# One extra multiply of ones ahead of the seven-product streams of four FFNs

## The chip, the cores and the metric

The kernel runs on one core of a Trainium2 chip. The metric is the device time of one execution in microseconds (us), median of several runs, lower is better. Three runs of the kernel before took 1838.65, 1840.2 and 1842.27 us; the median is 1840.2 us. Engines are named as in the profile: PE is the matrix engine (PEld its weight loads), DVE the vector engine, ACT the activation engine, POOL GpSimd, SP the engine that issues the weight transfers.

## The reference

Two batches of 256 tokens with 1024 channels go through a trunk of two layers with the same weights, so the kernel works on 512 tokens at once. Each layer is a half-step FFN, a token mixer, a second half-step FFN and a norm:

```python
def swiglu(x, w_gate, w_up, w_down):
    return (jax.nn.silu(x @ w_gate) * (x @ w_up)) @ w_down

for layer in range(DEPTH):                      # DEPTH = 2
    x = x + 0.5 * swiglu(rms_norm(x, ffn1_norm[layer]), ...)
    h = rms_norm(x, mix_norm[layer])
    x = x + mixer(h)                            # attention, another kind in each layer
    x = x + 0.5 * swiglu(rms_norm(x, ffn2_norm[layer]), ...)
    x = rms_norm(x, final_norm[layer])
```

The FFN's inner width is 2816, which is 22 chunks of 128. All is float32. The change touches only the four FFNs, called FFN1 to FFN4 here in order of time.

## The kernel before

**Products.** PE multiplies in a rounded float32 type, so every operand is split in a high and a low part (`wh`, `wl` for weights, `xh`, `xl` or pieces of `xb` for tokens), and each block product is three matmuls: `wh` by `xh`, `wh` by `xl`, `wl` by `xh`. ACT writes `wh` as a rounded copy, and DVE writes `wl` as the difference. Both read either a raw weight tile (`raw`, filled by a DMA on SP's queue, two buffers) or a sum of weight blocks (`T`, made by DVE).

**An FFN.** `ffn()` handles its 22 chunks in groups of 4, 6, 6 and 6 (`GROUPS`). For each chunk f it makes gate and up values, and after each group follows a down projection of that group (512-wide matmuls, `ba<-ah,wh` and the like, added up into X). The first chunks of an FFN (three in FFN1, two in the others, `PLAIN`) are made by plain 512-wide products. All other chunks take gate and up together by a Strassen-like scheme of seven products, numbered m = 1 to 7, on halves of the tokens: each has four blocks of 128 rows by three matmuls, which makes 12 matmuls of 256 columns. The products of a chunk run in the order 1, 3 (of the chunk before), 7, 6, 2, 5, 4. A group of six chunks is 42 products, 504 matmuls. In the first chunk by seven products (f = `PLAIN`) product 1 stands between the plain products, and the stream proper begins with product 6.

**Banks.** Products accumulate in banks of the matrix engine's result memory: `ba` (two, by chunk parity; products 1 and 2), `bg` (product 7), `bb` (two; products 4 and 6), `bc` (two; products 3 and 5). ACT copies `ba` into `bb` after product 1 and `bb` into `bc` after product 6, so that later products add to them; `gs<-bg` saves product 7; DVE forms `gate` and `us` from the banks, and the results are split into `ah` and `al` for the down projection. Products 1 and 7 begin with `start=True`, which overwrites the bank. An older piece, `begin()` (lines 877 to 880), multiplies a tile of ones by itself into the first halves of `bb` and `bc` at the start of each FFN, four matmuls of 256 columns.

**Order.** The order of PE's work is fixed by `ffn_order` (line 197 on). The order on ACT and DVE is worked out while the program is built: `Plan.run` (line 463 on) has an estimated clock per engine (`Clock`, `Engine.cost`), every PE product has a due time, and whichever ready task with the nearest due time is handed out next, weight copies (`emit_hi`), weight differences (`emit_lo`) and sums (`emit_sum`) among them. An engine runs its instructions strictly in the order so handed out, and waits at the first whose input is missing. The estimated clock advances with every call that goes through the `Engine` helper, so an extra matmul moves it too. All instructions show line 151, the helper's line.

Of the kernel before, what the change touches and what calls it, by code (L numbers as in the profile page):

```python
# [15 lines left out]
P = 128  # L16
# [5 lines left out]
GROUPS = (4, 6, 6, 6)  # L22
# [3 lines left out]
XSIDE = {1: 0, 7: 1, 2: 2, 4: 3, 6: 4, 3: 5, 5: 6}  # L26
# [3 lines left out]
PLAIN = {True: 3, False: 2}  # L30
# [512 lines left out]
def hybrid_trunk_kernel(ctx, tc, x, cst, wgu1, wd1, wgu2, wd2, win_ab, wout_ab, win_c, wout_c, ali, nab, y):  # L543
# [5 lines left out]
    PE = Engine(clock, "pe", nc.tensor)  # L549
# [11 lines left out]
    def acc(name):  # L561
        return clock.alloc(acc_p.tile([P, T], F32, tag="acc", name=name), "acc", BANKS["acc"])
# [72 lines left out]
    ones_r = per.tile([P, P], F32R, name="ones")  # L635
# [218 lines left out]
    def ffn(norm, nxt, index, groups, boundary=None, before=()):  # L854
        with tc.tile_pool(name="ffn", bufs=2, reuse_waits="tile") as fp:
            plan = Plan(clock, ws)
            l_first = bool(before)
            ba = [acc("ba") for _ in range(2)]
            bg = acc("bg")
            bb = [scp("bb") for _ in range(2)]  # L860
            bc = [trp("bc") for _ in range(2)]
            half = slice(0, 256)
# [7 lines left out]
            norm.more = [a.rearrange("p (k i t) -> p k i t", k=4, i=3) for a in shared("xb", F32R)]  # L870
            acts = {}
            part = {}

            steps = plan.steps
            steps(before)
# [8 lines left out]
            def when(do):  # L884
                later.append(do)
                if "S" in plan.writer:
                    while later:
                        later.pop(0)()
# [2 lines left out]

            def multiply(f, m, ps):
                wh, wl = ws.ready[index[f, WSIDE[m]]]
                for k in range(4):
                    w = slice(k * P, (k + 1) * P)
                    xh, xl = norm.block(XSIDE[m], k)
                    for j, (wt, xt) in enumerate(((wh, xh), (wh, xl), (wl, xh))):
                        PE.matmul(ps[:, half], lhsT=wt[:, w], rhs=xt, start=(m in (1, 7) and k == 0 and j == 0),
                                  stop=(k == 3 and j == 2), skip_group_check=True)

            def product_of(f, m):
                i = f % 2
                a, b, c = ba[i], bb[i], bc[i]
                ka, kb, kc = f"a{i}", f"b{i}", f"c{i}"
                gate, us, gs = f"gate{i}", f"us{i}", f"gs{i}"
                ps, key = {1: (a, ka), 2: (a, ka), 3: (c, kc), 4: (b, kb), 5: (c, kc), 6: (b, kb), 7: (bg, "g")}[m]
                p = index[f, WSIDE[m]]
                plan.add("pe", lambda: multiply(f, m, ps), [f"x{k}{XSIDE[m]}" for k in range(4)], [key], 1.404, (p, p + 1))
                if m == 1:
                    plan.add("act", lambda: A.activation(b[:, half], a[:, half], AF.Copy), [ka], [kb], 0.27)  # L910
                elif m == 7:
                    def keep():
                        part[f, "s"] = t = fp.tile([P, 256], F32, tag="gs", name="gs")
                        A.activation(t, bg[:, half], AF.Copy)
                    plan.add("act", keep, ["g"], [gs], 0.27)
                elif m == 6:
                    plan.add("act", lambda: A.activation(c[:, half], b[:, half], AF.Copy), [kb], [kc], 0.27)
                elif m == 2:
                    def scale():
                        part[f, "g"] = t = fp.tile([P, T], F32, tag="gate", name="gate")  # L920
                        V.tensor_tensor(t[:, half], a[:, half], norm.wide["s"][:, half], ALU.mult)
                    when(lambda: plan.add("dve", scale, [ka, "S"], [gate, gate + "b"], 0.34))
                elif m == 5:
                    def total():
                        part[f, "u"] = t = fp.tile([P, 256], F32, tag="us", name="us")
                        V.tensor_tensor(t, c[:, half], part[f, "s"], ALU.add)
                    plan.add("dve", total, [kc, gs], [us], 0.34)
                elif m == 4:
                    def total():
                        V.tensor_tensor(part[f, "g"][:, second], b[:, half], part.pop((f, "s")), ALU.add)  # L930

                    def scale():
                        t = part[f, "g"]
                        V.tensor_tensor(t[:, second], t[:, second], norm.wide["s"][:, second], ALU.mult)

                    def finish():
                        plan.add("dve", total, [kb, gs], [gate + "b"], 0.34)
                        plan.add("dve", scale, ["S"], [gate + "b"], 0.34)
                        plan.add("act", lambda: A.activation(part[f, "g"], part[f, "g"], AF.Silu), [],
                                 [gate, gate + "b"], 0.53)  # L940
                    when(finish)
                elif m == 3:
                    def times(s, what):
                        t = part[f, "g"]
                        V.tensor_tensor(t[:, s], t[:, s], what(), ALU.mult)

                    plan.add("dve", lambda: times(second, lambda: part.pop((f, "u"))), [us], [gate + "b"], 0.34)
                    plan.add("dve", lambda: times(half, lambda: c[:, half]), [kc], [gate], 0.34)
                    split_acts(f)
# [42 lines left out]
            def split_acts(f):  # L992
                gate = f"gate{f % 2}"

                def high():
                    t = fp.tile([P, T], F32R, tag="ah", name="ah", bufs=NA)
                    A.activation(t, part[f, "g"], AF.Copy)
                    part[f, "h"] = t

                def low():  # L1000
                    t = fp.tile([P, T], F32R, tag="al", name="al", bufs=NA)
                    h = part.pop((f, "h"))
                    V.tensor_tensor(t, part.pop((f, "g")), h.bitcast(F32), ALU.subtract)
                    acts[f] = (h, t)
                plan.add("act", high, [gate, gate + "b"], [f"ah{f % NA}"], 0.53)
                plan.add("dve", low, [f"ah{f % NA}", gate + "b"], [f"al{f % NA}", gate], 0.61)
# [88 lines left out]
            for slot, (kind, f, *m) in enumerate(order):  # L1095
                if slot == 3:
                    steps(stats)
                    steps(spread[:-2])
                    for k in range(4):
                        steps(norm.block_steps(k, room, False))  # L1100
                    late = [norm.block_steps(k, room, True) for k in range(4)]
                    for begun, _ in late:
                        steps(begun)
                if slot == 5:
                    steps(spread[-2:])
                    when(lambda: None)
                    steps(again[:-2])
                if slot == 6:
                    steps(again[-2:])
                if kind == "m" and f == n0 and m[0] == 6:  # L1110
                    for _, ended in late:
                        steps(ended)
                if kind == "m":
                    product_of(f, m[0])
                elif kind != "down":
                    plain(f, kind, m[0])
                else:
                    down(f, GROUPS[f], f0)
                    f0 += GROUPS[f]
            plan.run()  # L1120
            p = groups[-1][-1]
# [655 lines left out]
    before = [step for c in range(KC) for step in n.feed_steps(c)]  # L1777
    for l in range(2):
        for which in range(3):
            if which == 0:  # L1780
                nx = Norm(gains(1, l))
                ffn(n, nx, *ffn_parts[2 * l], gains(3, 0) if l == 1 else None, before if l == 0 else ())
            elif which == 1:
                nx = Norm(gains(2, l))
                (mixer_ab if l == 0 else mixer_c)(n, nx)
            else:
                if l == 0:
                    nx = Norm([comb[:, c:c + 1] for c in range(KC)], gains(3, 0))
                else:
                    nx = Last(gains(3, 1))  # L1790
                ffn(n, nx, *ffn_parts[2 * l + 1])
            n = nx
# [102 lines left out]
```

## Time and profile before

| | |
|---|---|
| runs, us | 1838.65, 1840.2, 1842.27 |
| profiled execution, us | 1841.28 |
| its span, us | 1839.5 |
| matmuls in the trace | 12412 |
| mean granted clock of PE | 0.992 |
| share of the span busy: PE, DVE, ACT, POOL | 97%, 83%, 52%, 8% |

The span is the time between the first and the last instruction of one profiled execution, in which all times of the trace are counted; 1.8 us lie around it. A row of the timeline has start, duration, engine, line, operation, `out<-in`, shapes and a count; matmuls are pipelined, so the duration of one overlaps the next, and the pace of a stream is read from one start to the next. A row of the chain of waits has start, duration and what held the end back at that time. The windows view gives, for each stretch, its length, the busy time of one engine with the count of its instructions, the granted clock of PE, and the DMA share.

Where the streams by seven products begin, in us: the first pairs of FFN1 to FFN4 at 49.1, 629.6, 976.3 and 1505.0; the groups behind a down projection at 79.4, 170.7 and 262.7 (FFN1), 673.9, 765.9 and 856.6 (FFN2), 1016.8, 1108.8 and 1200.8 (FFN3), 1548.9, 1640.9 and 1732.9 (FFN4).

### The profile page before, as it was taken

The page shows a single profiled execution, that of the slowest core. Times are in us where ns is not written, and L with a number is a line of the kernel's source. Part 1 is how long each engine was busy: PE and PEld are TensorE (multiplying, and loading weights), DVE is VectorE, ACT ScalarE, POOL GpSimd, SP SyncE. Part 2 cuts the span into 40 slices and gives each one's busy share as a digit, 9 for nine tenths or more (in the row PEclk, how much of TensorE's full clock was granted, in tenths as well). Part 3 has the DMA queues.
Part 4 walks back from the last instruction along what each step waited for, and adds up shares of the span by engine and source line. Part 5 has one row for each costly group of instructions (what it writes and reads, how often), then busy time and mean ns, then how long its engine had stood idle before and what let it go on. Part 6 is the DMA issues. An engine that isn't in the chain of part 4 may idle for free.

```text
span 1839.5 us, 31447 instructions
## 1 busy us (share of the span) xinstructions
PE 1792.9 (97%) x12412; PEld 1636.8 (89%) x12412; DVE 1523.3 (83%) x2849; ACT 964.0 (52%) x1975; POOL 155.8 (8%) x110
## 2 busy tenths in 40 slices
PE   8999999999899999999999999999998999999997
PEld 7998989898898889898978989898986788989896
DVE  8998888657876888888899989797877788888884
ACT  7463636445555646363664645455455664636362
POOL 0000000043431000000000000000344100000000
PEclk9999999999999999999999999999999999999999
DMA  4332323222212134242412332323111213414231
GB/s 151 126 126 82 125 82 125 96 92 70 81 70 97 53 104 138 69 141 69 140 65 92 110 120 87 121 86 125 49 70 47 72 47 112 138 69 138 69 115 46
DMA packets 31700, 175.53 MB, mean 95 GB/s; under 512 B 3392, under 2 KB 5696, under 8 KB 17088
## 3 DMA queue, kind: packets, MB, share of 16 engines
q1 hardware_dynamic: 31552, 173.52, 27.6%
q8 instruction: 97, 1.59, 0.4%
q14 instruction: 51, 0.42, 0.1%
HBM read 171.41 MB, written 2.10 MB: 94 GB/s over the span
## 4 chain that ended last, share of the span: by engine, by line
PE 70%; DVE 18%; ACT 6%; issue 3%; DMA 2%; POOL 1%; SPq 0%; POOLq 0%; DVEq 0%; ACTq 0%
PE ba L151 26%; PE bb L151 11%; PE bc L151 10%; PE bg L151 9%; PE ip L151 6%; DVE wl L151 5%; PE op L151 4%; ACT att L151 2%; DVE T L151 2%; DVE X L151 2%; DMA raw<-wd 1%; PE pv L151 1%; DVE dt L151 1%; DVE att L151 1%; DVE gate L151 1%
## 5 line engine op out<-in xcount | busy, mean ns | idle before, releaser
L151 ACT ACTIVATE wh<-raw 128x512 fp32r<-128x512 f32 x553 | 338.2, 626 | 233.9 <-PE bb L151 69.3
L151 DVE TENSOR_TENSOR wl<-raw,wh 128x512 fp32r<-128x512 f32 x516 | 371.3, 727 | 64.5 <-ACT wh L151 57.2
L151 ACT ACTIVATE wh<-T 128x512 fp32r<-128x512 f32 x316 | 198.1, 630 | 273.9 <-PE ba L151 130.7
L151 PE MATMUL bc<-xb,wh 128*128 128x256 f32 x1264 | 231.2, 282 | 5.6 <-DVE us L151 5.0
L151 DVE TENSOR_TENSOR wl<-T,wh 128x512 fp32r<-128x512 f32 x316 | 215.5, 686 | 21.8 <-ACT wh L151 18.5
L151 PE MATMUL ba<-xh,wh 128*128 128x256 f32 (+1 forms) x704 | 206.5, 293 | 4.5 <-ACT wh L151 4.5
L151 PE MATMUL ba<-al,wh 128*128 128x512 f32 (+1 forms) x534 | 206.6, 387 | 0.5 <-DVE al L151 0.5
L151 PE MATMUL ba<-ah,wh 128*128 128x512 f32 (+1 forms) x534 | 206.8, 387 | 0.0
L151 PE MATMUL ba<-ah,wl 128*128 128x512 f32 (+1 forms) x534 | 206.4, 386 | 0.0
L151 PE MATMUL ba<-xh,wl 128*128 128x256 f32 (+1 forms) x704 | 206.3, 293 | 0.0
L151 PE MATMUL ba<-xl,wh 128*128 128x256 f32 (+1 forms) x704 | 206.2, 293 | 0.0
L151 PEld LDWEIGHTS bc<-xb,wh 128*128 128x128 f32 x1264 | 193.3, 189 | 7.2 <-DVE us L151 5.6
L151 PE MATMUL bc<-xb,wl 128*128 128x256 f32 x632 | 177.6, 281 | 0.0
L151 PE MATMUL ip<-wh,xh 128*128 128x256 f32 x576 | 166.9, 290 | 0.0
L151 PE MATMUL ip<-wh,xl 128*128 128x256 f32 x576 | 161.6, 281 | 0.6 <-DVE xl L151 0.6
L151 PE MATMUL ip<-wl,xh 128*128 128x256 f32 x576 | 161.4, 280 | 0.0
L151 PEld LDWEIGHTS ba<-xh,wh 128*128 128x128 f32 x704 | 132.7, 189 | 8.5 <-ACT wh L151 4.7
L151 PEld LDWEIGHTS ba<-xh,wl 128*128 128x128 f32 x704 | 134.6, 191 | 3.9 <-DVE wl L151 0.5
L151 PEld LDWEIGHTS ba<-xl,wh 128*128 128x128 f32 x704 | 132.9, 189 | 3.9
L151 PEld LDWEIGHTS bc<-xb,wl 128*128 128x128 f32 x632 | 121.3, 192 | 0.0
L151 PEld LDWEIGHTS ba<-al,wh 128*128 128x128 f32 x534 | 100.9, 189 | 20.7 <-DVE al L151 0.9
L151 PEld LDWEIGHTS ba<-ah,wl 128*128 128x128 f32 x534 | 100.7, 189 | 20.2
(200 smaller groups left out, 4371.9 us busy)
## 6 DMA issues: line engine op xcount, KB each, us to landing
raw<-wgu SPq DMA_DIRECT2D x87, 1024.0 KB, 4.8
raw<-wd SPq DMA_DIRECT2D x48, 768.0 KB, 4.2
raw<-win_ab SPq DMA_DIRECT2D x12, 1024.0 KB, 4.8
raw<-wd SPq DMA_DIRECT2D x16, 512.0 KB, 3.7
raw<-win_c SPq DMA_DIRECT2D x6, 1024.0 KB, 4.8
raw<-wout_ab SPq DMA_DIRECT2D x4, 1024.0 KB, 4.8
raw<-wout_c SPq DMA_DIRECT2D x4, 1024.0 KB, 4.8
X<-x SPq DMA_DIRECT2D x8, 256.0 KB, 5.2
```

The lines of the kernel that those rows point to most:

```text
L151: return f(*args, **kw)
```

## The change

At 16 places, four in each FFN, one matmul of 256 columns is put ahead: ones by ones, with `start=True, stop=True`. Ahead of product 1 of the first chunk of groups 2, 3 and 4 it goes to the same half of `ba` that product 1 then overwrites; ahead of product 6 of the first chunk by seven products it goes to `bg`, which product 7 of that chunk overwrites. Nothing that is read later depends on it.

```diff
+            begins = [(sum(GROUPS[:g]), 1) for g in range(1, len(GROUPS))] + [(PLAIN[bool(before)], 6)]
...
             def multiply(f, m, ps):
                 wh, wl = ws.ready[index[f, WSIDE[m]]]
+                if (f, m) in begins:
+
+                    PE.matmul((ps if m == 1 else bg)[:, half], lhsT=ones_r, rhs=ones_r.unsqueeze(1).to_broadcast([P, 2, P]),
+                              start=True, stop=True, skip_group_check=True)
                 for k in range(4):
...
-                plan.add("pe", lambda: multiply(f, m, ps), [f"x{k}{XSIDE[m]}" for k in range(4)], [key], 1.404, (p, p + 1))
+                plan.add("pe", lambda: multiply(f, m, ps), [f"x{k}{XSIDE[m]}" for k in range(4)], [key, "g"] if (f, m) in begins and m == 6 else [key],
+                         1.404, (p, p + 1))
```

The extra matmul goes through the helper `PE`, so the estimated clock moves by its cost (256 / 2190 = 0.117 us), and some tasks of ACT and DVE are handed out in another order. POOL's and SP's orders and those of the mixers stay as they were. The rows below name tiles as above; a number behind `wh`, `wl`, `raw` or `T` is a running number of that build, which differs between the two kernels for the same tile, and a name in square brackets is the engine or DMA queue that the instruction waits for.

PE, at the head of a group, here the second group of FFN1 (at 79.4 us). Before:

```order
L151 MATMUL ba<-ah,wh_671 128x512
L151 MATMUL ba<-al,wh_671 128x512
L151 MATMUL ba<-ah,wl_675 128x512
L151 MATMUL ba<-xh,wh_705 128x256 [waits DVE_49,Activation_49]
L151 MATMUL ba<-xl,wh_705 128x256
L151 MATMUL ba<-xh,wl_719 128x256
```

and now:

```order
L151 MATMUL ba<-ah,wh_672 128x512
L151 MATMUL ba<-al,wh_672 128x512
L151 MATMUL ba<-ah,wl_676 128x512
L151 MATMUL ba<-ones 128x256 [waits DVE_49]
L151 MATMUL ba<-xh,wh_706 128x256 [waits Activation_49]
L151 MATMUL ba<-xl,wh_706 128x256
L151 MATMUL ba<-xh,wl_720 128x256
```

The extra matmul stands between the last 512-wide matmul of the down projection and the first of product 1; it takes over the wait for DVE (the bank must have been read), and the wait for ACT (`wh`) stays with product 1. At the first pairs the extra `bg<-ones 128x256` stands in the same way, without a wait, between the last plain product (`bb<-xh,wl`) and the first matmul of product 6 (`bb<-xb,wh`).

DVE, in the first chunks by seven products of FFN2 (at 636 us); FFN4 has the same rows at 1512 us. Before:

```order
L151 TENSOR_TENSOR gate<-ba,S 128x256 [waits DVE_49,PE_49]
L151 TENSOR_TENSOR wl_7382<-T_7332,wh_7354 128x512 [waits Activation_49]
L151 TENSOR_TENSOR us<-bc,gs 128x256 [waits PE_49,Activation_49]
L151 TENSOR_TENSOR wl_7400<-raw_6991,wh_7356 128x512
L151 TENSOR_TENSOR al<-gate,ah 128x512
```

and now:

```order
L151 TENSOR_TENSOR gate<-ba,S 128x256 [waits DVE_49,PE_49]
L151 TENSOR_TENSOR wl_7387<-T_7337,wh_7359 128x512 [waits Activation_49]
L151 TENSOR_TENSOR wl_7403<-raw_6995,wh_7361 128x512 [waits Activation_49]
L151 TENSOR_TENSOR us<-bc,gs 128x256 [waits PE_49,Activation_49]
L151 TENSOR_TENSOR al<-gate,ah 128x512
```

The difference `wl` that is the last to read its raw tile now stands ahead of `us`, and with it the moment at which that tile is free for the next transfer.

ACT, at the end of the second group of FFN3 (at 1070 us). Before:

```order
L151 ACTIVATE gs<-bg 128x256 [waits PE_49]
L151 ACTIVATE bc<-bb 128x256 [waits PE_49]
L151 ACTIVATE wh_12457<-raw_12377 128x512 [waits DMAHW5_49]
L151 ACTIVATE wh_12459<-raw_12377 128x512
L151 ACTIVATE wh_12474<-raw_12377 128x512 [waits PE_49]
```

and now:

```order
L151 ACTIVATE gs<-bg 128x256 [waits PE_49]
L151 ACTIVATE wh_12453<-raw_12375 128x512 [waits DMAHW5_49]
L151 ACTIVATE wh_12467<-raw_12375 128x512 [waits PE_49]
L151 ACTIVATE bc<-bb 128x256 [waits PE_49]
L151 ACTIVATE wh_12484<-raw_12375 128x512 [waits PE_49]
```

The copy of product 6 into `bc`, to which product 5 adds, now stands behind two weight copies, the first of which waits for a DMA.

## The prediction

> **What bounds the kernel now.** I read the page first, then the chain of waits inside the FFNs, then PE's timeline at the 16 places that the change touches, and last the windows.
>
> ```profile
> span 1839.5 us, 31447 instructions
> PE 1792.9 (97%) x12412; PEld 1636.8 (89%) x12412; DVE 1523.3 (83%) x2849; ACT 964.0 (52%) x1975; POOL 155.8 (8%) x110
> ...
> PE 70%; DVE 18%; ACT 6%; issue 3%; DMA 2%; POOL 1%; SPq 0%; POOLq 0%; DVEq 0%; ACTq 0%
> ```
>
> PE sets the end for 70% of the span, with matmul after matmul, so what counts is the pace of its streams. DVE's 18% lie at the beginnings of FFNs. The chain inside two groups of FFN2 shows the same product of 12 matmuls with two prices:
>
> ```profile
> 774.50 1.36 PE ba L151 x12
> ...
> 858.17 1.41 PE bg L151 x12
> ```
>
> One group runs at 1.36 us a product, the next at 1.41 us, and neither waits for anything. Stretches of 42 us in the middle of groups, in PE's windows (length, busy, count, clock, DMA), count it better; the first and last slow ones and the only fast one:
>
> ```profile
> 174.00:216.00 42.00, 42.00 (x359) 1.00 0.30 97
> ...
> 774.00:816.00 42.00, 42.00 (x373) 1.00 0.36 128
> ...
> 1736.00:1778.00 42.00, 42.00 (x359) 1.00 0.29 96
> ```
>
> Nine groups (those at 170.7, 262.7, 673.9, 856.6, 1108.8, 1200.8, 1548.9, 1640.9 and 1732.9) have 359 matmuls in such a stretch, one has 373, at the same granted clock of 1.00 and without idle time. The pace, 113 ns or 118 ns from start to start, is therefore a state of the stream, and it is kept for a whole group. How is it entered? A group's head comes straight from 512-wide matmuls:
>
> ```profile
> 856.37 0.39 PE L151 MATMUL ba<-ah,wl 128*128 128x512 f32 x1
> 856.59 0.28 PE L151 MATMUL ba<-xh,wh 128*128 128x256 f32 x1
> 856.71 0.28 PE L151 MATMUL ba<-xl,wh 128*128 128x256 f32 x1
> ```
>
> All 12 heads look like this and begin with 0.12 us a matmul, the slow pace. The fast stretch began elsewhere, at a small wait:
>
> ```profile
> 771.53 0.47 PE L151 MATMUL bc<-xb,wh 128*128 128x256 f32 x2
> 771.83 0.28 PE L151 MATMUL bc<-xb,wl 128*128 128x256 f32 x1
> ...
> 1042.19 0.44 PE L151 MATMUL bc<-xb,wh 128*128 128x256 f32 x2
> 1042.47 0.28 PE L151 MATMUL bc<-xb,wl 128*128 128x256 f32 x1
> ```
>
> Two matmuls took 0.30 and 0.28 us here where two at the slow pace take 0.24, and behind both places the stream was fast; I count 14 entries after a wait in the FFNs, 12 of them fast. So the entry decides.
>
> **The extra multiplies.** Sixteen matmuls, each 0.113 to 0.118 us (the rows above), together 1.8 to 1.9 us, if nothing hides them. The two ends are 0 and 1.9. In FFN1 and FFN3 the first pair and the first group behind a down projection run beside a DVE that sets the time:
>
> ```profile
> 79.00:138.00 59.00, 56.20 (x107) 1.00 0.40 134
> ...
> 977.68 1.80 DVE wl L151 x3
> ```
>
> The first row is DVE's window (95% busy), the second one of a chain that from 976 to 990 us names almost DVE alone; PE waits for it later, so these four cost nothing. Those at 629.6 and 1505.0 are followed by a wait of over 2 us (below) that takes them in. Six hidden, ten on the path: **+1.2 us**; uncovered, +1.9.
>
> **The pace.** The extra matmul changes the entry of each stream: other weights, another moving operand, and one matmul more between the 512-wide stream and the products. The trace has one like it, the ones of `begin`, which also follow 512-wide matmuls:
>
> ```profile
> 1479.57 0.39 PE L151 MATMUL op<-mh,wl 128*128 128x512 f32 x1
> 1479.80 0.40 PE L151 MATMUL bb<-ones 128*128 128x256 f32 x2
> 1480.03 0.40 PE L151 MATMUL bc<-ones 128*128 128x256 f32 x2
> 1480.27 0.40 PE L151 MATMUL ba<-xh,wh 128*128 128x512 f32 x1
> ```
>
> The first two take 0.23 us to the next start, the second two 0.24: the first step is a little shorter than at a group's head, so the stream behind is shifted, but the ones themselves go on slowly. That speaks for a changed entry and leaves open where four ones lead against one. If the entry changes, the products can only go to the other of the two paces that the trace has, so for the nine slow groups it is bounded by 0 and by the full difference. A group is 42 products of 1.41 us, 59.2 us; at the fast pace it lasts 359/373 of that, 2.2 us less. Nine groups: **-20.0 us**. I take the full end as the likelier, since all 12 identical entries gave one state and most other entries the other.
>
> Part comes back at the end of each fast group, where the chain through DVE, the weight DMA and ACT, which a slow group hides, comes last. The fast group shows it:
>
> ```profile
> 816.38 0.28 PE L151 MATMUL bg<-xh,wl 128*128 128x256 f32 x1
> 816.64 0.50 PE L151 MATMUL bb<-xb,wh 128*128 128x256 f32 x2
> 816.99 0.28 PE L151 MATMUL bb<-xb,wl 128*128 128x256 f32 x1
> ...
> 819.37 0.28 PE L151 MATMUL ba<-xh,wl 128*128 128x256 f32 x1
> 819.74 0.51 PE L151 MATMUL bc<-xb,wh 128*128 128x256 f32 x2
> 820.08 0.28 PE L151 MATMUL bc<-xb,wl 128*128 128x256 f32 x1
> ```
>
> From 816.38 to 816.99 are three steps in 0.61 us instead of 0.34, from 819.37 to 820.08 three in 0.71: 0.27 + 0.37 = 0.64 us a group. Nine times: **+5.8 us**, between 0 and that.
>
> [...]
>
> **The moved instructions.** In FFN2 and FFN4 DVE's last `wl` on a raw tile now stands ahead of `us`. In the chain of FFN2:
>
> ```profile
> 636.67 0.34 DVE us L151
> 637.01 0.61 DVE wl L151
> ...
> 637.67 3.66 DMA raw<-wd
> ...
> 643.34 3.86 DMA raw<-wd
> ...
> 648.57 0.34 DVE us L151
> ...
> 648.96 1.90 PE bc L151 x12
> ```
>
> `us` at 636.67 lies on it, delays the transfer by 0.34 us, and everything up to PE's restart hangs on that transfer. Without it PE starts 0.34 us sooner, in FFN4 as well (same rows, and this wait): **-0.7 us**.
>
> ```profile
> PE bc L151 <- DVE us L151: 2.2, 1, 2.2
> ```
>
> If ACT, which then waits for the earlier transfer, were late itself, 0. Behind this wait stands a stretch at half clock:
>
> ```profile
> 650.00:654.00 4.00, 4.00 (x15) 0.57 0.74 266
> ```
>
> Here 3.4 us did the work of 1.7. A shorter wait could spare that, in both FFNs 3.4 us at most. [...] I take 0 and keep -3.4 for the range.
>
> In FFN3, on ACT, `bc<-bb` now stands behind two copies, the first waiting for a transfer:
>
> ```profile
> 1070.19 0.37 ACT L151 ACTIVATE bc<-bb 128x256 f32<-128x256 f32 x1
> 1071.87 1.68 ACT L151 ACTIVATE wh<-raw 128x512 fp32r<-128x512 f32 x3 [1.31 <-DMA raw<-wd]
> ```
>
> The three copies start 0.53 us apart, so `bc<-bb` comes at about 1072.9 instead of 1070.19 and is done at 1073.3. PE's product 5 needs it:
>
> ```profile
> 1071.25 0.39 PE L151 MATMUL bc<-xb,wh 128*128 128x256 f32 x2
> ...
> 1074.67 0.50 PE L151 MATMUL bc<-xb,wh 128*128 128x256 f32 x2 [0.53 <-DVE us L151]
> ```
>
> It moves from 1071.25 to about 1073.35; product 4 behind it ends at 1076.07, and product 3 starts then instead of at 1074.67, its own wait gone: **+1.4 us**, 0 if the transfer lands 2 us earlier, 2.1 if nothing behind takes any of it. The other exchanges on ACT and DVE stand where PE runs from a lead, and I cost them at nothing; such a lead gone would cost what one wait above does, 0.3 us. The mixers and the last 24 us are untouched.
>
> **Sum**, against the execution's own 1841.28 us: +1.2 - 20.0 + 5.8 - 0.7 + 1.4 = -12.3, 1829.0 us. That execution lies 1.1 us above the median of the runs, so I say **1828 us**.
>
> **The rivals.** *The pace doesn't turn*: the stream behind one multiply of ones settles at 118 ns as it does behind four. For it speaks that the ones ran at 0.24 a pair; against it, that the first step differs. Left: 1.2 - 0.7 + 1.4 = +1.9, 1843.2, as a median **1842**. *Half of it turns*, or the chain behind takes more than 0.64 us: five of nine groups give 5 × (2.2 - 0.64) = 7.8, with +1.9 that is 1835.4, as a median **1834**. *The existing fast stretches are lost*: they start at small waits like the one at 771.53, and the new order on ACT and DVE can remove these, while the heads stay slow. Two of them, at 771.5 and at 1042.2, feed some 37 and 22 fast products, 59 × 0.05 = 3.0 us; less the 0.64 us at the end of the first and about as much in the second, 1.8 to 2.4 on top of 1842: **1844**. It decides from both waits vanishing; for it speaks that the wait at 771.53 is only 0.06 us long (0.30 against 0.24), against it that three quarters of the heads have none to lose.
>
> **How the numbers follow.** A measurement of this kernel can tell about 0.2% (3.7 us) from no change, so faster means below 1836.5 and slower above 1843.9. The forecast gets 0.55, half of it 0.08 (both faster), no turn 0.28 (same), the lost stretches and other mishaps past 1843.9 0.09. The lower end is the forecast with no wait at the ends of half the groups and the clock windows spared, 1828 - 2.9 - 3.4, with room for the unhidden parts about 1821; I take 1820. The upper end takes in no turn with all 16 multiplies uncovered, 1842 + 0.7, and part of the slower case: 1843.8. The forecast's own range is 1820 to 1833.
>
> **What will show it.** In the windows view a 42 us stretch of each group has 373 matmuls instead of 359, and the chain's products read 1.36; if it still has 359, the pace step is wrong. Heads show one `ba<-ones` of about 0.115 us and no wait. At the ends of groups two small waits on `bb` and `bc`. In FFN2 and FFN4 the restart of `bc` after the long wait comes 0.3 us earlier against the beginning of its FFN, and in FFN3 `bc<-bb` stands behind the copies with PE waiting for ACT instead of for `us`. The prediction is wrong if the heads turn only in some groups, if a turned group loses its 2.2 us at its end, or if an order change makes a wait that I costed at nothing.

## The result and the profile after

| | before | after |
|---|---|---|
| median of the runs beside each other, us | 1839.49 (4 runs, 1838.65 to 1842.27) | 1818.62 (4 runs, 1816.35 to 1820.6) |
| profiled execution, us | 1841.28 | 1817.23 |
| its span, us | 1839.5 | 1815.5 |
| mean granted clock of PE | 0.992 | 0.996 |

The ratio is 0.9883, 95% interval 0.9871 to 0.9895: 1.2% faster, 20.9 us by the medians. The forecast was 1828 us with a range from 1820 to 1843.8; the sign came as forecast and the pace turned, the gain is 1.7 times what was forecast, and the time lies 1.4 us below the range.

The page of the profile after, same rows as before:

```profile
span 1815.5 us, 31467 instructions
PE 1772.1 (98%) x12428; PEld 1616.8 (89%) x12428; DVE 1517.2 (84%) x2849; ACT 959.4 (53%) x1975; POOL 155.9 (9%) x110
...
PE 78%; DVE 12%; ACT 5%; issue 2%; DMA 1%; POOL 1%; SPq 0%; POOLq 0%; ACTq 0%; DVEq 0%
```

There are 16 matmuls more and 20.8 us less of busy PE. PE holds 78% of the chain, and DVE's share fell from 18% to 12%. PE's windows of 42 us in the middle of four groups (length, busy, count, clock, DMA):

```profile
174.00:216.00 42.00, 42.00 (x367) 1.00 0.31 104
265.00:307.00 42.00, 42.00 (x373) 1.00 0.32 106
...
850.00:892.00 42.00, 42.00 (x365) 1.00 0.33 110
...
1716.00:1758.00 42.00, 42.00 (x373) 1.00 0.33 114
```

The fast count, 373, stands in seven of ten groups read so; those at 174, 850 and 1101 us have 367, 365 and 372. The chain of waits of the second of these three tells why:

```profile
867.71 1.36 PE bb L151 x12
869.07 1.36 PE ba L151 x12
870.43 1.48 PE bc L151 x12
871.91 1.41 PE bb L151 x12
```

It ran at 1.36 us a product until a small wait at 870.4, where the product lasted 0.12 us longer, and at 1.41 behind it: a fall back to the slow pace in the middle of a group. At the heads PE's timeline shows the extra matmul without a wait:

```profile
845.42 0.39 PE L151 MATMUL ba<-ah,wl 128*128 128x512 f32 x1
845.64 0.28 PE L151 MATMUL ba<-ones 128*128 128x256 f32 x1
845.76 0.28 PE L151 MATMUL ba<-xh,wh 128*128 128x256 f32 x1
```

The stage table below is worked out from the first matmul of each stage to the first of the next in PE's timeline. "Group" is a group behind a down projection with its extra matmul; "first chunks" run from the ones of `begin` to the end of the down projection that follows.

```
stage            before us   after us   difference
FFN1 groups      58.63 59.36 59.36   57.88 58.41 57.26   -0.75 -0.94 -2.10
FFN2 groups      59.36 58.06 59.36   57.26 57.26 58.61   -2.10 -0.81 -0.75
FFN3 groups      59.43 59.36 59.36   59.36 57.91 57.26   -0.08 -1.45 -2.10
FFN4 groups      59.36 59.36 59.36   57.26 57.26 57.26   -2.10 -2.10 -2.10
FFN2 first chunks      69.44               67.13               -2.32
FFN3 first chunks      68.16               68.11               -0.05
FFN4 first chunks      69.11               67.36               -1.75
first mixer           249.75              247.61               -2.14
second mixer          186.97              186.22               -0.75
```

The twelve groups give 17.4 us, the first chunks of FFN2 and FFN4 4.1 us, the mixers 2.9 us; with the small rest that is the 24.0 us between the two spans.

### The profile page after: what moved, and what is told of

It is laid out like the page before. It is cut to its first block, busy times and chain, and to the rows that moved or that the text cites. A ratio compares the mean times of both kernels' runs of the same rounds, so it can differ in the third digit from the quotient of the medians.

```text
span 1815.5 us, 31467 instructions
## 1 busy us (share of the span) xinstructions
PE 1772.1 (98%) x12428; PEld 1616.8 (89%) x12428; DVE 1517.2 (84%) x2849; ACT 959.4 (53%) x1975; POOL 155.9 (9%) x110
## 4 chain that ended last, share of the span: by engine, by line
PE 78%; DVE 12%; ACT 5%; issue 2%; DMA 1%; POOL 1%; SPq 0%; POOLq 0%; ACTq 0%; DVEq 0%
PE ba L151 30%; PE bb L151 13%; PE bc L151 12%; PE bg L151 11%; PE ip L151 6%; PE op L151 4%; DVE wl L151 2%; ACT att L151 2%; DVE att L151 1%; PE pv L151 1%; DVE X L151 1%; DVE nm L151 1%; DVE dt L151 1%; DMA raw<-wd 1%; DVE xl L151 1%
## 5 line engine op out<-in xcount | busy, mean ns | idle before, releaser
L151 PE MATMUL bc<-xb,wh 128*128 128x256 f32 x1264 | 225.7, 278 | 3.7 <-DVE us L151 3.2
```

Source lines behind the costliest of these rows:

```text
L151: return f(*args, **kw)
```

## The experiments

Fifteen kernels, each a small edit of the kernel after, and the kernel after once more. A head that has turned is told by its group: 57.26 us against 59.36, or 59.48 with an extra matmul that did nothing.

### The order alone, and the multiplies alone

`order_only` charges the planner's clock for the extra matmuls and doesn't issue them, so that ACT and DVE have the order of after and PE has the program of before:

```diff
-                    PE.matmul((ps if m == 1 else bg)[:, half], lhsT=ones_r, rhs=..., start=True, stop=True, ...)
+                    o = (ps if m == 1 else bg)[:, half]
+                    clock.issue("pe", 256 / 2190, [o], [ones_r, ones_r.unsqueeze(1).to_broadcast([P, 2, P])])
```

> The order of DVE and ACT of the change, without the multiplies (their cost is charged to the planner's clock alone). If the multiply turns the pace: all 12 heads stay at 118 ns, full groups last 59.36 us, and the time is that of before, 1838 to 1842 us. If the order alone brings part of the gain: below 1836 us, seen in the first chunks of FFN2 and FFN4 (0.3 us each, and 1.7 us more where the half-clock stretch is gone).

Measured: 1840.58 us, ratio 1.0006 (0.9997 to 1.0016). The nine slow groups stayed slow, as a window of `order_only` shows:

```profile
174.00:216.00 42.00, 42.00 (x359) 1.00 0.28 95
```

The order gains 2.2 us in the first chunks of FFN2 and loses as much elsewhere: FFN1's first group lasts 1.06 us longer and FFN2's second 1.30, because the small wait at 771.5, at which that group used to turn fast, is gone, and it stays at 118 ns to its end. So the mechanism of my third rival exists; the multiply at the head outweighs it.

`keep_order` issues the multiplies but doesn't charge the clock (ACT and DVE have the order of before):

```diff
-                    PE.matmul(
+                    nc.tensor.matmul(
```

> The 16 multiplies as in the change, but not charged to the planner's clock, so that DVE and ACT have the order of before. If the pace of PE's streams is the whole gain: the 12 heads turn to 113 ns, groups that wait for nothing last 57.26 us instead of 59.36, and the time is within 2 us of the change's (1817 to 1821 us). If the new order matters: the small waits at 771 us or the wait chain at the ends of groups come back, some heads relapse, and up to 6 us of the gain are lost (1821 to 1827 us). In FFN2 and FFN4 the restart behind the long wait should come 0.34 us later than in the change.

Measured: 1821.66 us, ratio 0.9907 (0.989 to 0.9923). Its heads turn:

```profile
174.00:216.00 42.00, 42.00 (x373) 1.00 0.32 106
```

The multiplies alone carry the gain: in its profile the nine formerly slow groups gained 18.3 us, against 15.7 in the change. PE's restart in FFN2 and FFN4 came 0.52 and 0.21 us later than in the change, counted from the ones of `begin`, where 0.34 was expected. Whether the new order adds something on top of them (0.9883 against 0.9907, with intervals that touch) isn't settled; alone it brought nothing.

### Which property of the extra matmul turns the pace

`twin` (a copy of the first real matmul), `ones_by_x` (ones as weights, the tokens moving):

```diff
-   lhsT=ones_r, rhs=ones_r.unsqueeze(1).to_broadcast([P, 2, P])
+   lhsT=wh[:, 0:P], rhs=norm.block(XSIDE[m], 0)[0]          # twin
+   lhsT=ones_r, rhs=norm.block(XSIDE[m], 0)[0]              # ones_by_x
```

> The extra matmul is a copy of the first real one (same weights, same tokens), overwritten; both waits then stand on the copy. If any extra matmul turns the pace: 12 heads at 113 ns, groups of 57.3 us. If it takes an operand that is unlike the stream's, or the wait of the bank and that of the weights on two different matmuls: the stream only begins one matmul sooner, all heads stay at 118 ns, full groups last 59.4 to 59.5 us, and the time is 1839 to 1844 us.

> The extra matmul has ones as weights and the real tokens as moving operand; the bank's wait stands on it, the weights' wait on the next one, as in the change. If the ones as weights or the parted waits turn the pace: 12 heads at 113 ns, groups of 57.3 us, 1816 to 1822 us. If it is the moving ones (one tile read twice): heads stay at 118 ns, full groups last 59.5 us.

Measured: `twin` 1840.08 us in one run, with full groups of 59.48 us; `ones_by_x` 1819.85 us in one run, with seven of the nine groups at 57.26. The same window of `twin` and then of `ones_by_x`:

```profile
174.00:216.00 42.00, 42.00 (x359) 1.00 0.27 95
```

```profile
174.00:216.00 42.00, 42.00 (x373) 1.00 0.32 106
```

One more matmul was not enough, and with ones as weights it made no difference here whether ones or tokens moved (57.26 us for a group that ran through, in the change as in `ones_by_x`). Two properties were left, the ones as weights, and that the two waits now stand on two instructions. Three kernels part them:

```diff
-   lhsT=ones_r, rhs=ones_r.unsqueeze(1).to_broadcast([P, 2, P])
+   lhsT=norm.block(0, 0)[0][:, 0:P], rhs=norm.block(0, 0)[0]                # x_by_x
+   lhsT=ones_r, rhs=wh[:, 0:256]                                           # ones_by_w
+   lhsT=wh[:, 0:P], rhs=ones_r.unsqueeze(1).to_broadcast([P, 2, P])        # w_by_ones
```

> Extra matmul with tokens as weights and tokens as moving operand; the bank's wait (DVE) stands on it, the weights' wait (ACT) on the first real matmul. If the parted waits turn the pace: 12 heads at 113 ns, groups without a wait 57.26 us, time 1816 to 1823 us. If it is the tile of ones as weights: heads stay at 118 ns, groups 59.48 us, time 1838 to 1843 us.

> Extra matmul with ones as weights and a piece of the new weight tile as moving operand, so that both waits (DVE and ACT) stand on the extra matmul, and the first real one waits for nothing. If the parted waits turn the pace: heads stay at 118 ns, groups 59.48 us, 1838 to 1843 us. If it is the ones as weights: heads at 113 ns, groups 57.26 us, 1816 to 1823 us.

> Extra matmul with the new weight tile as weights and ones as moving operand; both waits on it. By the parted waits, and by the ones as weights: heads stay at 118 ns, groups 59.48 us, 1838 to 1843 us. If any moving operand unlike the stream's does it: 113 ns and 57.26 us.

Measured, one run each: `x_by_x` 1820.33 us, `ones_by_w` 1818.76, `w_by_ones` 1838.01. `ones_by_w` has both waits on the extra matmul, as they stood on the first one before, and all its heads turn; the groups that run through take 57.25 us (the last one fell back behind a wait of 0.4 us and took 59.60). The full groups of `w_by_ones` take 59.48. The parted waits are out: here it hangs on the weights. `x_by_x`, with tokens as weights, turned as well. One of its heads, FFN2's first, began behind a wait of 0.4 us; the other eleven followed the last 512-wide matmul as in the change, with the same steps (table below). So ones are not special here: a tile of tokens did the same, with 373 matmuls in the 42 us from 1716 us on.

Next, whether the extra load only has to differ from the following one (`w_other_block`: the second 128 columns of the same tile), and whether two ones do the same:

```diff
+   lhsT=wh[:, P:2 * P], rhs=norm.block(XSIDE[m], 0)[0]      # w_other_block
...
+                    for _ in range(2):                      # two_ones, heads only
+                        PE.matmul(... ones ...)
```

> As the copy of the first matmul, but with the second 128 columns of the same new weight tile as weights: same kind of tile, same waits, another block than the next load. If the pace turns whenever the extra load differs from the next one: heads at 113 ns, groups 57.26 us, 1816 to 1823 us. If it needs a tile of another shape (ones, tokens): heads stay at 118 ns, groups 59.48 us, 1838 to 1843 us.

> Two multiplies of ones ahead of each of the 12 groups, none at the first pairs. In the change the load behind the ones' load came 225.0 ns after it, in the kernels that did not turn 226.8 ns. If only the change from one block to another shortens that step: the second of the two does it as the first did alone, heads at 113 ns, groups 57.37 us, 1818 to 1824 us. If each load behind ones is early, the two steps add up to another position and the pace may stay at 118 ns: 1839 to 1844 us.

Measured: `w_other_block` 1835.89 us in one run, seven of the nine slow groups at 59.48 and no head turned (its profile has one half-clock stretch in the middle of the kernel where before has four, which at 1.5 to 1.7 us each is, as an estimate, most of its low time; see below); `two_ones` 1823.46 us, seven of nine at 57.37. Another block of `wh` was not enough, and a second multiply of ones cost its 0.11 us a group and left the heads fast. Three more about the tile:

```diff
+   lhsT=wl[:, 0:P], rhs=norm.block(XSIDE[m], 0)[0]                           # wl_tile
...
-    ones_r = per.tile([P, P], F32R, name="ones")
+    ones_r = wp.tile([P, P], F32R, tag="ones", name="ones", bufs=1)          # ones_in_ring_pool
...
+   PE.matmul(ps[:, 0:64], lhsT=ones_r, rhs=ones_r[:, 0:64], ...)             # ones_64, heads only
```

> Extra matmul with the first block of wl of the same chunk as weights, a tile of the same ring of buffers in the same memory pool as wh, with the waits parted as in the change. If any tile but wh, or the parted waits, turns the pace: heads at 113 ns, groups 57.26 us. If tiles of the weight rings never do, only ones and tokens: heads stay at 118 ns, groups 59.48 us, 1836 to 1843 us.

> The change with the tile of ones kept in the memory pool of the weight rings instead of the pool of the tokens. If the place of the tile decides: heads stay at 118 ns, groups 59.48 us, 1836 to 1843 us. If not: heads at 113 ns, groups 57.26 us, 1816 to 1823 us.

> Only the 12 group heads, each with 64 moving columns instead of 256. If the load of another tile is what turns the pace: groups of about 57.2 us (0.06 less than with 256 columns), 1816 to 1822 us. If the length of the step from the extra matmul to the first real one matters: heads stay at 118 ns, groups 59.4 us, 1836 to 1842 us.

Measured: `wl_tile` 1839.54 us and `ones_in_ring_pool` 1843.35 us in one run each, `ones_64` 1842.06 us with a ratio of 1.0011 (1.0 to 1.0022). The heads of none turned. `ones_in_ring_pool` is the kernel after in every instruction and in every order; the tile of ones lies elsewhere, and tiles set up behind it in either pool may have moved with it, since no trace shows addresses. The last windows of `ones_in_ring_pool` and of `ones_64`:

```profile
1736.00:1778.00 42.00, 42.00 (x359) 1.00 0.27 95
```

```profile
1740.00:1782.00 42.00, 42.00 (x359) 1.00 0.29 96
```

Was it the pool? `ones_first` keeps the tile in its old pool and allocates it there first, which by the code moves the pool's tiles in front of its old place by one tile's size (no trace shows addresses):

```diff
+    ones_r = per.tile([P, P], F32R, name="ones")
     cs = per.tile([P, NPER + 24], F32, name="cs")
...
-    ones_r = per.tile([P, P], F32R, name="ones")
```

> The change with the tile of ones kept in its old pool but ahead of all other tiles of that pool, so that it lies elsewhere, at the pool's beginning. If what decides is whether the tile lies in the rings' pool: heads at 113 ns, groups 57.26 us, 1816 to 1823 us. If each place has its own outcome: it may stay at 118 ns, groups 59.48 us, 1836 to 1843 us, and then the turn in the change is an accident of this layout.

Measured: 1843.18 us in one run, all full groups at 59.47 or 59.48:

```profile
174.00:216.00 42.00, 42.00 (x359) 1.00 0.28 96
```

So it isn't the pool either: the same matmul of the same ones turned the heads with one layout of the tiles out of three. Whether the place of the ones decides or that of the tiles that moved with them isn't parted. The mean steps from one matmul's start to the next at the 12 heads, worked out from the trace's nanosecond starts (first the step from the last 512-wide matmul; for `x_by_x` the eleven heads without a wait):

```
kernel              steps in ns
before              226.4  117.6  117.4  118.6  117.2  117.8  118.1
twin                226.4  117.6  117.4  118.6  117.2  117.8  118.2
after               226.0  117.2  116.8  117.4  122.6  118.2  113.4
ones_by_w           225.8  117.4  123.2  118.5  113.2  113.2  113.5
x_by_x              225.9  117.4  116.7  117.5  122.4  118.4  113.5
two_ones            225.8  115.7  118.5  121.5  115.8  114.2  113.5
ones_in_ring_pool   226.8  113.2  118.4  119.3  117.2  118.4  117.5
ones_first          225.7  117.6  114.1  118.3  117.6  117.4  117.6
ones_64             225.7   29.3  201.3  116.7  117.7  117.3  118.3
```

The copy of the first matmul leaves every step as it was. Ones as weights shift the steps by 1 to 6 ns in all cases (`ones_64` apart, whose extra matmul is shorter). In all nine profiles whose heads turned, each head of the table has one step of 121 to 124 ns, and the stream goes on at 113; in the heads that stayed slow, `ones_64` apart, no step between two matmuls of 256 columns is over 120 ns. So the long step goes with the turn; that it is the cause is not shown. What a tile's place does to these steps the trace doesn't tell, and it stays open.

### Where else it would help, and the change once more

`heads_only` leaves out the four first pairs (the same list without `(PLAIN[bool(before)], 6)`). `heads_and_mixers` puts one multiply of ones, besides the 12 heads, ahead of the first input projection of each mixer. `change_again` is the kernel after, on the chip of `heads_and_mixers`.

```diff
         ps = acc("ip")
+        if not hasattr(norm, "begun"):
+            norm.begun = True
+            PE.matmul(ps[:, 0:256], lhsT=ones_r, rhs=ones_r.unsqueeze(1).to_broadcast([P, 2, P]), ...)
```

> Only the 12 multiplies ahead of the groups, none ahead of the first pairs. If the multiply at the first pairs brings nothing (in the change all four first pairs ran at 118 ns behind it, two of them at 113 ns before): as fast as the change or up to 2 us faster, 1815 to 1820 us, and the first pairs of FFN3 and FFN4 at 1.36 us a product again. If they matter through the order of DVE and ACT: 1820 to 1824 us.

> The 12 multiplies ahead of the groups and one ahead of the first input projection of each mixer, where 317 and 237 matmuls in a row ran at 118 ns behind a down projection (none at the first pairs). If an unlike load turns any 256-wide stream behind a 512-wide one: 1.4 us less in the first mixer, 1.0 in the second, 1814 to 1819 us, 1 to 3 us below the change. If these streams, which load tokens as weights, keep their pace: the same as the change within 1 us.

> The change itself on the same chip as the kernel above: 1816 to 1821 us. The six or more groups without a wait last 57.26 us again; which of the others fall back to 118 ns behind a small wait, or wait at their ends for a long transfer, may differ from the first profile.

Measured: `heads_only` 1819.43 us, ratio 0.9895 (0.9878 to 0.9911), the same as the change as far as this can be told: the four multiplies at the first pairs bring nothing. They did not leave these streams alone, though. PE's windows of 6 us at FFN4's first pair, in before and after:

```profile
1505.10:1511.10 6.00, 6.00 (x56) 1.00 0.31 87
```

```profile
1489.10:1495.10 6.00, 6.00 (x53) 1.00 0.30 87
```

and in `heads_only`, which has no multiply there, and in `ones_first`, which has one:

```profile
1491.90:1497.90 6.00, 6.00 (x55) 1.00 0.28 87
```

```profile
1508.00:1514.00 6.00, 6.00 (x56) 1.00 0.31 87
```

In before the first pairs of FFN3 and FFN4 were fast; in the change all four are slow. With ones or tokens as weights in the layout of the change (both its profiles, `keep_order`, `ones_by_x`, `ones_by_w`, `x_by_x`) all 24 first pairs ran at 117.8 ns a matmul. In `ones_in_ring_pool` and `ones_first`, whose heads stayed slow, all eight ran at 113.4. Without an extra matmul there, in six kernels, 13 of 24 were fast; with a weight tile as weights, in four, six of 16. So in these three layouts the multiply sets the pace, but to the fast one at the heads and the slow one at the first pairs, or the other way round. It cost nothing there that the times show: FFN3's first chunks took 68.16 us before and 68.11 after.

`heads_and_mixers` 1822.17 us, 0.9903 (0.9887 to 0.9919); `change_again` 1817.2 us, 0.9876 (0.9861 to 0.9891). The mixer's stream, which loads tokens as weights, kept its pace, first in `heads_and_mixers`, then in the kernel before:

```profile
359.00:385.00 26.00, 26.00 (x223) 1.00 0.41 142
```

```profile
359.00:385.00 26.00, 26.00 (x224) 1.00 0.39 130
```

No version beat the change. In the second profile of the change eight of the nine formerly slow groups last 57.26 to 57.40 us, against seven of nine groups below 58 in the first, and the group at 170 us, which had fallen back there, ran through: where a group fell back differed between these two executions, except in FFN2's last group, which fell back at the same product in both.

## Why the prediction was wrong, point by point

The pace turned as forecast, and the time still came out below the range, because three terms were sized wrongly. The return at the ends of groups was put at +5.8 us; the nine groups gave back 3.2 and 1.5 us in the two profiles of the change, none of it by the waits that I priced. The half-clock stretches in FFN2 and FFN4 were left at 0; both were gone in both profiles, 3.2 us. FFN3's +1.4 us came out as -0.08.

**The pace (right in mechanism and nearly in size).** "All 12 identical entries gave one state and most other entries the other" led to the full end, 2.2 us a group. A group that ran through gained 2.10 us with its extra matmul, so 2.22 without. `twin` shows that the reason I gave was too wide: one matmul more doesn't change the entry. Ones as weights did in the layout of the change, and in two other layouts they didn't, which nothing in the trace of before could have told. That the heads turned here was so far luck. And the turn went both ways: the same multiply slowed the first pairs of FFN3 and FFN4 (FFN4's from 56 to 53 matmuls in 6 us), a loss that my sum doesn't name.

**The return at the ends of groups, +5.8 us (the step that failed most).** I took the two waits at 816 and 819 us for the price of any fast group. The groups that ran through in the change have none at all, FFN2's second among them, and ran at 1.36 us to the end. The chain behind the waits, in before and then in `ones_by_x`, which waited there as well:

```profile
809.14 5.42 DMA raw<-wd
```

```profile
799.74 5.48 DMA raw<-wd
```

The timeline of SP's queue (start, length of the stretch in which it handled the four weight transfers of that down projection) of before, after and `ones_by_x`:

```profile
801.29 17.04 SPq L288 DMA_DIRECT2D raw<-wd  x4
```

```profile
790.99 15.66 SPq L288 DMA_DIRECT2D raw<-wd  x4
```

```profile
791.89 17.10 SPq L288 DMA_DIRECT2D raw<-wd  x4
```

The two with the waits have a transfer of 5.4 to 5.5 us in the chain, where the page's median is 4.2, and a stretch 1.4 us longer than the change, which has neither. Before and the nine profiles whose heads turned divide by it: in six (`ones_by_w`, `heads_only`, `two_ones` and `heads_and_mixers` besides these two) the stretch took 16.8 to 17.1 us, and each waited at the end of this group; in four (both profiles of the change, `keep_order`, `x_by_x`) it took 15.6 to 15.7, and none waited. Transfers of `wd` over 5 us were rare, none to three of 64 in each of these ten traces. I priced a slow transfer at one place as a property of the pace. What the nine groups did give back is another thing: falls back to the slow pace behind small waits, 1.2, 1.4 and 0.7 us in the first profile. Forecast for the nine groups with their multiplies was 13.1 us, measured 15.7 in the first profile and 17.4 in the second.

**FFN1's and FFN2's other groups (left out).** I counted no gain where a part was already fast. FFN2's second group gained 0.81 us in both profiles. FFN1's first, led by DVE, gained 0.75 in one and lost 0.51 in the other.

**The first chunks of FFN2 and FFN4, -0.7 us.** Measured -2.3 and -1.75. Counted from the ones of `begin`, PE's restart came 0.67 us earlier in FFN2 and 0.22 us in FFN4, together 0.9 where 0.7 was forecast. In FFN2 the wait before it fell from 2.3 us to

```profile
PE bc L151 <- DVE us L151: 1.5, 1, 1.5
```

The larger part, 1.65 us in FFN2 and 1.54 in FFN4, lies behind the restart: it is the half-clock stretch, which is missing in both (clock 0.57 in before from 650 to 654 and from 1524 to 1528 us, 1.00 in after from 640 to 646 and from 1505 to 1511 us). `order_only` shows nearly all of the gain in FFN2 (0.58 + 1.65 us) with the moved `wl` and no multiply; in FFN4 its wait was 2.1 us, and the stretch stayed. All 18 profiles together bear the reading out: at these two places none of the 20 waits of up to 1.83 us had a half-clock stretch behind it, and 11 of the 16 waits from 1.87 to 2.44 us had one. I named that end (-3.4 for both) and took 0.

**FFN3, +1.4 us.** Measured -0.08, and +0.05 in `order_only`, which has the same order and slow heads. ACT's timeline after shows why:

```profile
1058.05 0.62 ACT L151 ACTIVATE wh<-raw 128x512 fp32r<-128x512 f32 x1
1058.83 0.63 ACT L151 ACTIVATE wh<-raw 128x512 fp32r<-128x512 f32 x1 [0.16 <-PE bb L151]
1059.37 0.37 ACT L151 ACTIVATE bc<-bb 128x256 f32<-128x256 f32 x1
```

The first copy starts right behind `gs` and waits for no transfer; `bc<-bb` comes 1.3 us later than right behind it, not 2.7. I had kept the landing of before, and that was an accident of one execution. The transfers that end there, in the DMA view of before (1060 to 1076 us) and of after (1048 to 1065 us), with the median time to landing at the end of the row:

```profile
raw<-wd SPq DMA_DIRECT2D x3, 768.0 KB, 5.2
```

```profile
raw<-wd SPq DMA_DIRECT2D x3, 768.0 KB, 4.1
```

Two in a row took 5.21 and 6.18 us in before; in the other 17 profiles the same two took 3.8 to 4.3 us. The second landed 55.1 us behind the group's head in before, 52.9 in after, and 53.1 in `keep_order`, which has the order of before: the prediction's own condition for 0, a landing 2 us earlier, was the usual case.

**The extra multiplies, +1.2 us.** As forecast: 0.12 us at each head; those at the first pairs cost nothing that the table shows and bring nothing, though they slowed two of these streams.

**The mixers, 0.** They were 2.9 us shorter in the profile after, which the multiplies don't explain: `w_other_block`, whose heads didn't turn, has the first mixer 2.1 us shorter too. It is half-clock stretches again, for the larger part. Rows of PE's windows before, and at the same place after:

```profile
503.30:506.90 3.60, 3.60 (x20) 0.53 0.00 0
```

```profile
500.00:504.00 4.00, 4.00 (x37) 1.00 0.02 4
```

**The range.** The bounds were in the text: no waits at the ends (-5.8), FFN3 at 0 (-1.4), both half-clock stretches spared (-3.4) give 1817.4, below the measured median. I took half of the first and the whole of the third, which gives 1821.7, left out the second, and set 1820. The forecast's clock windows are these two stretches, 3.41 us long at a clock of 0.50; what sets their length and place no run shows. Of the 24 us between the two profiled executions, some 3 are such luck of the one execution, since the medians lie 20.9 us apart.

## What to carry to other kernels

Where long streams of equal matmuls stand, read the pace from start to start for each stretch and ask how each stretch was entered; here two paces 4% apart, 113.4 and 117.8 ns a matmul at the same granted clock of 1.00, were worth 16 to 17 us in the nine slow groups. A turn found in this way belonged here to one layout and one kind of entry: the matmul that made the group heads fast made the first pairs slow. After any change of tiles the pace of each stream has to be read again, and a copy of the next matmul is a good control. And a wait seen once in one execution is no price per group: look first whether a transfer in its chain was longer than the median.

## What the runs showed of the hardware

- A 256-wide stream of load and multiply pairs ran at 113.4 ns or 117.8 ns a matmul, at a granted clock of 1.00, and kept either for 500 matmuls. An extra matmul ahead with ones or tokens as weights set the pace, in the layout of the change to 113.4 at the heads and 117.8 at all 24 first pairs; with ones in the two other layouts it was 117.8 at the heads and 113.4 at all eight first pairs. A stream also turned either way at small waits: to fast behind 771.5 us in before, where two matmuls took 0.30 us instead of 0.24, and to slow behind 870.4 us in after, where a product lasted 0.12 us longer.
- The same group of four transfers took 15.66 us in after, 17.04 in before, and 17.10 in `ones_by_x`, which has the orders of after on ACT and DVE. Single transfers of 768 KB, 4.1 to 4.2 us at the median of a page, took up to 6.18 us.
- In the middle of the kernel (without its beginning and its end) the profile before had four half-clock stretches of 3.41 us at a clock of 0.50, the first profile of the change had none, its second profile had one, `keep_order` three. In FFN2 and FFN4 each cost 1.5 to 1.7 us. In these profiles they stood behind waits of PE of 1.9 to 3.1 us; in FFN2 and FFN4 of all 18 profiles none followed a wait of up to 1.83 us. A good part of the spread of about 4 us between executions of one kernel may come from them, an estimate from that cost and those counts; it was not tested by itself.
